# Splitting transposed probabilities straight from PSUM, and moving small steps between VectorE and GpSimd, in a two-layer encoder kernel

## The chip, the cores and the metric

The kernel runs on one core of a Trainium2 chip. The metric is device time of one execution in microseconds (us); runs of the kernel before took 3246.87 us in the median (3243.1 to 3257.06 over 3 runs). Engines are named PE (TensorE, matrix products and transposes), DVE (VectorE), ACT (ScalarE), POOL (GpSimd) and SP (SyncE, which issues the DMAs). PSUM is the memory that PE writes its products to; POOL doesn't read it in this kernel.

## The reference

Input x is 1024 x 1024 in float32. Each of two layers does

```
h    = rmsnorm(x) ; proj = h @ w_in          # 2464 columns for four head groups
A: 4 heads of width 64, 2 key/value heads, normed and rotated q and k, softmax attention
B: 4 heads, differential: softmax(q1 k1 + bias) - lam * softmax(q2 k2 + bias), times v, then a norm
C: 4 heads, low-rank q, k and v, width 96, softmax attention
D: 4 heads, three dilated windows, each with its own softmax, combined by their log-sum-exp
x    = x + concat(A, B, C, D) @ w_out
u    = depthwise width-3 convolution of rmsnorm(x) @ w_up
x    = x + (silu(gate) * val) @ w_down
```

The bias of B and D is a slope times the distance of query and key, -slope * |i - j|, and D also masks keys outside its windows.

## The kernel before, in words

Every matrix product takes operands in fp32r. To keep precision an operand is split into a high part (the value cast to fp32r) and a low part (the value less the high part), and a product is the sum of two or three products of parts.

A layer runs in this order: norm and projection of the columns of B and C (`norm1`, `proj`), then the attention stream, then the MLP. The stream (`stream`, line 414) is a list of events at numbered positions. Within a position events come in the classes SOFT, STEP, SC, EXP, AV, SET, and after them a filler (`fill`): during B the rest of the input projection (`inproj`, for A and D), then the output projection of heads that are done (`out_stage`). Groups come in the order B, C, D, A, with 64, 64, 32 and 64 positions. In B, C and A a pair of query blocks of 128 takes four positions, one step each.

For a pair in B, `sc` (line 645) makes scores of 128 x 1024 in PSUM, in two buffers, for two query blocks and two halves of the head. `mx` (652) adds the bias table, writes P to SBUF and its row maximum, and a second instruction (660) scales the maximum by -slope for the exponential. `ex` (662) is the exponential on ACT with its row sum. `comb` (667), once per query block, at two successive positions, turns sums into factors and adds the second half's P, scaled, to the first (675). In A and C (`dense`, 533) the maximum (550) and the exponential (556) need no bias table. In D (`head_D`, 712) `mx` and `ex` (785, 798) are as in B at 128 x 256, and `finish_D` combines the windows.

`step` (480) is common to all groups. Four transposes by PE put a 128 x 512 piece of P^T in a PSUM bank of the pool `pt` (two buffers; stacks of q and k, line 441, and the small products `o`, line 521, take their banks from the same pool). ACT copies it to `pf` in SBUF. The high part is a cast from `pf` by DVE (492), or for the steps listed in `h_act` a second reading of PSUM by ACT (490). The low part is a subtraction by POOL from `pf` (493). `products` (496) multiplies both parts by v two positions later. `h_act` holds two of four steps in A and B, one of four in C and none in D.

`head_norm` (207) norms q and k: square on ACT, sum on DVE, 1/root on POOL (`rstd`, 108), the product with it on DVE (216), the gain on POOL (218). `by_act` is False while `inproj` runs. `vsplit` (473) splits v: high part on ACT, low part on DVE (helper `split`, line 130).

The order of PE's instructions is the program's (`manual_schedule`, line 1253). The order of DVE, ACT and POOL is drawn up by the framework from its own timeline when the program is built (line 1295). Semaphores are set by the framework.

## Time and profile before

| | |
|---|---|
| runs | 3257.06, 3246.87, 3243.1 us |
| profiled execution | 3249.78 us |
| its span | 3248.0 us |
| PE busy | 3064.0 us, 94% |
| DVE busy | 2042.5 us, 63% |
| ACT busy | 1480.5 us, 46% |
| POOL busy | 1441.2 us, 44% |
| mean granted clock of TensorE | 0.972 |

The profile is of one execution. The span goes from its first to its last instruction. Shares are means over stages that differ much, so the stages are read one by one. A group of instructions in the profile has a line, an engine, an operation, output <- inputs by the program's names, shapes and a count; behind them stand its busy time, the mean time of one, and the idle time of the engine in front of them with what ended it. A row of a stretch holds its start and end, its length, then busy time and number of instructions of PE, PE's weight loads, DVE, ACT and POOL, the mean granted clock, the share of the DMA engines' time and GB/s. A name such as `P<-P,r2b` leaves the buffer's number out.

### The profile page before, as it was taken

The page shows a single profiled execution, that of the slowest core. Times are in us where ns is not written, and L with a number is a line of the kernel's source. Part 1 is how long each engine was busy: PE and PEld are TensorE (multiplying, and loading weights), DVE is VectorE, ACT ScalarE, POOL GpSimd, SP SyncE. Part 2 cuts the span into 40 slices and gives each one's busy share as a digit, 9 for nine tenths or more (in the row PEclk, how much of TensorE's full clock was granted, in tenths as well). Part 3 has the DMA queues.
Part 4 walks back from the last instruction along what each step waited for, and adds up shares of the span by engine and source line. Part 5 has one row for each costly group of instructions (what it writes and reads, how often), then busy time and mean ns, then how long its engine had stood idle before and what let it go on. Part 6 is the DMA issues. An engine that isn't in the chain of part 4 may idle for free. (4 is left out here: it accounts for less than half of the span.)

```text
span 3248.0 us, 44899 instructions
## 1 busy us (share of the span) xinstructions
PE 3064.0 (94%) x16800; PEld 2637.4 (81%) x16800; DVE 2042.5 (63%) x3596; ACT 1480.5 (46%) x2813; POOL 1441.2 (44%) x1128
## 2 busy tenths in 40 slices
PE   7988899799999999999989888997999999999999
PEld 5978888688888888888769788886888888888887
DVE  6789976676734444444566999766767344444445
ACT  5567776556732212222154667765567222221221
POOL 2368775645632222223122677755456322222221
PEclk9999999899999999999999899998999999999999
DMA  4332241221311111111133312412213111111111
GB/s 145 112 105 57 62 132 43 67 62 50 47 54 46 52 46 46 52 46 52 50 113 112 102 51 63 132 44 68 60 49 47 59 39 52 46 52 46 49 49 65
DMA packets 276874, 213.05 MB, mean 66 GB/s; under 512 B 197168, under 2 KB 242608, under 8 KB 276656
## 3 DMA queue, kind: packets, MB, share of 16 engines
q1 hardware_dynamic: 276656, 210.18, 22.4%
q8 instruction: 132, 2.16, 0.3%
q14 instruction: 86, 0.70, 0.1%
HBM read 157.70 MB, written 41.94 MB: 61 GB/s over the span
## 5 line engine op out<-in xcount | busy, mean ns | idle before, releaser
L141 PE MATMUL u<-h2T,wu 128*128 128x512 f32 x4224 | 1013.7, 392 | 0.0
L141 PEld LDWEIGHTS u<-h2T,wu 128*128 128x128 f32 x4224 | 792.3, 188 | 179.8
L493 POOL TENSOR_TENSOR PT<-pf,PT 128x512 fp32r<-128x512 f32 x448 | 599.1, 1342 | 392.3 <-DVE PT L492 240.7
L975 DVE TENSOR_TENSOR xacc<-xacc,d 128x1024 f32<-128x1024 f32 x352 | 424.5, 1217 | 460.2 <-PE d L141 459.7
L141 PE MATMUL d<-wd,gt 128*128 128x512 f32 x2112 | 525.7, 392 | 4.1 <-DVE xacc L975 4.1
L141 PE MATMUL pj<-w,hT 128*128 128x256 f32 (+2 forms) x3072 | 497.5, 316 | 24.7 <-ACT w L134 11.7
L130 POOL TENSOR_TENSOR wu<-rawu,wu 128x1024 fp32r<-128x1024 f32 x88 | 212.6, 2417 | 655.7 <-ACT wu L134 655.7
L141 PEld LDWEIGHTS pj<-w,hT 128*128 128x128 f32 x3072 | 445.2, 197 | 53.9 <-ACT w L134 13.4
L141 PEld LDWEIGHTS d<-wd,gt 128*128 128x128 f32 x2112 | 394.7, 188 | 97.0 <-DVE xacc L975 10.8
L944 ACT ACTIVATE c<-u,cw 128x1024 f32<-128x1024 f32 x88 | 106.3, 1207 | 527.9 <-PE u L141 527.8
L488 ACT COPY pf<-pt 128x512 f32<-128x512 f32 x448 | 261.8, 585 | 134.1 <-PE pt L145 109.9
L145 PE MATMUL pt<-cst,P 128*128 128x128 f32 x1792 | 285.7, 284 | 35.4 <-DVE q L464 13.4
L945 DVE SCALAR_TENSOR_TENSOR c<-u,cw,c 128x1023 f32<-128x1023 f32 x88 | 112.9, 1283 | 297.0 <-ACT c L944 296.9
L141 PEld LDWEIGHTS ot<-PT,v 128*128 128x128 f32 x1664 | 260.5, 196 | 46.2 <-POOL PT L493 15.1
L141 PE MATMUL ot<-PT,v 128*128 128x256 f32 x1664 | 282.0, 291 | 8.1 <-POOL PT L493 8.0
L145 PEld LDWEIGHTS pt<-cst,P 128*128 128x128 f32 x1792 | 219.2, 146 | 60.6 <-DVE q L464 16.4
L130 POOL TENSOR_TENSOR wd<-rawd,wd 128x1024 fp32r<-128x1024 f32 x44 | 105.6, 2400 | 289.6 <-ACT wd L134 289.6
L141 PE MATMUL S<-k,q 96*128 96x512 f32 (+2 forms) x512 | 215.2, 445 | 6.8 <-DMA k<-k 5.8
L492 DVE CAST PT<-pf 128x512 fp32r<-128x512 f32 x288 | 163.6, 568 | 64.9 <-ACT pf L488 58.5
L141 PE MATMUL od<-wo,mT 128*128 128x512 f32 x768 | 201.1, 401 | 2.8 <-DVE mT L1024 1.6
L664 ACT ACTIVATE P<-P,nmb 128x1024 f32<-128x1024 f32 x128 | 147.2, 1151 | 103.1 <-DVE nmb L660 102.7
L550 DVE TENSOR_REDUCE nm<-S 128x1 f32<-128x1024 f32 x128 | 156.2, 1220 | 32.7 <-PE S L141 31.2
(202 smaller groups left out, 4199.3 us busy)
## 6 DMA issues: line engine op xcount, KB each, us to landing
rawu<-in_w_up_dram SPq DMA_DIRECT2D x88, 512.0 KB, 3.3
rawd<-in_w_down_dram SPq DMA_DIRECT2D x44, 512.0 KB, 3.3
rawi<-in_w_in_dram SPq DMA_DIRECT2D x20, 512.0 KB, 3.9
rawo<-in_w_out_dram SPq DMA_DIRECT2D x16, 512.0 KB, 3.3
sC<-cqk SPq DMA_DIRECT2D x16, 384.0 KB, 2.4
ld<-sB SPq DMA_DIRECT2D x24, 256.0 KB, 3.6
sD<-pe SPq DMA_DIRECT2D x48, 128.0 KB, 1.7
ld<-sC SPq DMA_DIRECT2D x16, 384.0 KB, 3.5
```

What stands on the lines that cost most here:

```text
L130: eng.tensor_tensor(dst[1], src, dst[0].bitcast(F32), op=ALU.subtract)
L141: self.nc.tensor.matmul(out, l, r, start=start, stop=stop)
L145: self.nc.tensor.transpose(out, in_, self.ident[:p, :p])
L488: nc.scalar.copy(pf, pt)
L492: nc.vector.tensor_copy(PT[:, 0, :], pf)
L493: nc.gpsimd.tensor_tensor(PT[:, 1, :], pf, PT[:, 0, :].bitcast(F32), op=ALU.subtract)
L550: nc.vector.tensor_reduce(nm, Ps["S", i], axis=AX.X, op=ALU.max, negate=True)
L664: nc.scalar.activation(P, P, AF.Exp, bias=jb["nm", i][:, s:s + 1], scale=slope, accum_out=jb["ss", i][:, s:s + 1])
L944: nc.scalar.activation(c, u, AF.Identity, scale=cw[:, 1, jj:jj + 1], bias=cw[:, 3, jj:jj + 1])
L945: nc.vector.scalar_tensor_tensor(c[:, 1:], u[:, :S - 1], cw[:, 0, jj:jj + 1], c[:, 1:], op0=ALU.mult, op1=ALU.add)
L975: nc.vector.tensor_tensor(xacc[:, t, :], xacc[:, t, :], d, op=ALU.add)
```

## The change

Seven edits:

1. In `step`, ACT casts the high part straight from PSUM for every step, and DVE subtracts it from PSUM for the low part. `pf`, the cast by DVE and the subtraction by POOL go; so does `h_act`. PT has four buffers in place of three.
2. In B and D, the sum of scores and table is multiplied by -slope in the instruction that takes the maximum, which becomes a minimum. It is used as the exponential's bias as it stands; the separate scaling goes (64 instructions per layer in B, 64 in D).
3. `comb` runs once per pair, at the later of its two positions, with two reciprocals of two columns and one narrow product for both query blocks. The two wide products are the same.
4. The product of `head_norm` with 1/root is on POOL while `by_act` is False.
5. The low part of v is on POOL.
6. `finish_D` follows edit 2 (minimum, sign).
7. The tiles of sums and maxima in B are per pair, with two buffers.

```diff
--- before.py
+++ after.py
@@ -213,7 +213,7 @@
         ss = sp.tile([128, nh], F32, tag="hss", name="hss")
         nc.vector.tensor_reduce(ss, sv, axis=AX.X, op=ALU.add)
         r = self.rstd(sp, ss, d, nh, "hr")
-        nc.vector.tensor_tensor(dst, src, bc(r.unsqueeze(2), [128, nh, d]), op=ALU.mult)
+        (nc.vector if self.by_act else nc.gpsimd).tensor_tensor(dst, src, bc(r.unsqueeze(2), [128, nh, d]), op=ALU.mult)
         if gain is not None:
             nc.gpsimd.tensor_tensor(dst, dst, gain, op=ALU.mult)
 
@@ -473,27 +473,22 @@
     def vsplit(self, pos, src, c0, dst, n=NT, tag="v"):
         def go():
             t = (self.dp if n > NT else self.ac).tile([128, n, 128], F32R, tag=tag, name=tag, bufs=1 if n > NT else 2)
-            self.split((t[:, :, 0:64], t[:, :, 64:128]), src["t"][:, :n, c0:c0 + 64])
+            self.split((t[:, :, 0:64], t[:, :, 64:128]), src["t"][:, :n, c0:c0 + 64], "act", "pool")
             dst["t"] = t
         self.ev(pos, self.SET, go)
 
-    def step(self, cols, box, h_act=False):
+    def step(self, cols, box):
 
         nc = self.nc
         pt = self.pt.tile([128, 512], F32, tag="pt", name="pt")
         for o, ap in cols:
             self.T(pt[:, o:o + 128], ap)
         PT = self.ac.tile([128, 2, 512], F32R, tag="PT", name="PT", bufs=self.n_PT)
-        pf = self.ac.tile([128, 512], F32, tag="pf", name="pf", bufs=2)
-        nc.scalar.copy(pf, pt)
-        if h_act:
-            nc.scalar.copy(PT[:, 0, :], pt)
-        else:
-            nc.vector.tensor_copy(PT[:, 0, :], pf)
-        nc.gpsimd.tensor_tensor(PT[:, 1, :], pf, PT[:, 0, :].bitcast(F32), op=ALU.subtract)
+        nc.scalar.copy(PT[:, 0, :], pt)
+        nc.vector.tensor_tensor(PT[:, 1, :], pt, PT[:, 0, :].bitcast(F32), op=ALU.subtract)
         box["PT"] = PT
 
-    def products(self, g, Ps, v, done, h_act, late=0):
+    def products(self, g, Ps, v, done, late=0):
 
 
         lag, nc = 2, self.nc
@@ -502,7 +497,7 @@
             box = {}
             self.ev(g + kp, self.STEP, lambda kp=kp, box=box: self.step(
                 [(kk * 256 + i * 128, Ps[i][:, (2 * kp + kk) * 128:(2 * kp + kk + 1) * 128])
-                 for kk in range(2) for i in range(2)], box, kp in h_act))
+                 for kk in range(2) for i in range(2)], box))
 
             def mms(kp=kp, box=box):
                 if kp == 0:
@@ -570,7 +565,7 @@
                     self.mix_job(h, j, mb["m"][:, 2 * j:2 * j + 2, :])
                 elif j == 3:
                     self.mix_out(h, mb["m"])
-            self.products(gj, Ps, v, done, (1, 3) if C == "A" else (3,))
+            self.products(gj, Ps, v, done)
         return 16
 
     def mix_job(self, h, j, mix):
@@ -650,44 +645,44 @@
                     self.mm(ps[:, ks], qs_[s]["t"][0:96, qb * 128:(qb + 1) * 128], ks_[s]["t"][0:96, ks], True, True)
 
             def mx(i, s, j=j, Ps=Ps, jb=jb):
-                if s == 0:
-                    jb["ss", i] = at.tile([128, 2], F32, tag="ssb", name="ssb", bufs=3)
-                    jb["nm", i] = at.tile([128, 2], F32, tag="nmb", name="nmb", bufs=3)
+                if s == 0 and i == 0:
+                    jb["ss"] = at.tile([128, 2, 2], F32, tag="ssb", name="ssb", bufs=2)
+                    jb["nm"] = at.tile([128, 2, 2], F32, tag="nmb", name="nmb", bufs=2)
                 P = Ps[i, s] = at.tile([128, S], F32, tag="P", name="P", bufs=self.n_P)
-                o, nm = (7 - 2 * j - i) * 128, jb["nm", i][:, s:s + 1]
-                nc.vector.tensor_tensor_reduce(out=P, in0=Ps["S", i, s], in1=self.toep[:, o:o + S], scale=1.0, scalar=NEG,
-                                               op0=ALU.add, op1=ALU.max, accum_out=nm)
-                nc.vector.tensor_scalar(nm, nm, -slope, None, op0=ALU.mult)
+                o = (7 - 2 * j - i) * 128
+                nc.vector.tensor_tensor_reduce(out=P, in0=Ps["S", i, s], in1=self.toep[:, o:o + S], scale=-slope, scalar=-NEG,
+                                               op0=ALU.add, op1=ALU.min, accum_out=jb["nm"][:, s, i:i + 1])
 
             def ex(i, s, Ps=Ps, jb=jb):
                 P = Ps[i, s]
-                nc.scalar.activation(P, P, AF.Exp, bias=jb["nm", i][:, s:s + 1], scale=slope,
-                                     accum_out=jb["ss", i][:, s:s + 1])
-
-            def comb(i, j=j, Ps=Ps, jb=jb):
-                if j == 0 and i == 0:
+                nc.scalar.activation(P, P, AF.Exp, bias=jb["nm"][:, s, i:i + 1], scale=-1.0,
+                                     accum_out=jb["ss"][:, s, i:i + 1])
+
+            def comb(j=j, Ps=Ps, jb=jb):
+                if j == 0:
                     mb["rs"] = at.tile([128, NT], F32, tag="rsb", name="rsb")
-                qb, ss = 2 * j + i, jb["ss", i]
+                ss = jb["ss"]
                 r2 = at.tile([128, 2], F32, tag="r2b", name="r2b")
-                nc.vector.reciprocal(r2, ss)
-                nc.vector.tensor_copy(mb["rs"][:, qb:qb + 1], r2[:, 0:1])
-                nc.vector.scalar_tensor_tensor(r2[:, 1:2], r2[:, 1:2], ss[:, 0:1], self.nlam, op0=ALU.mult, op1=ALU.mult)
-                nc.vector.scalar_tensor_tensor(Ps[i, 0], Ps[i, 1], r2[:, 1:2], Ps[i, 0], op0=ALU.mult, op1=ALU.add)
-                Ps[i] = Ps[i, 0]
+                nc.vector.reciprocal(mb["rs"][:, 2 * j:2 * j + 2], ss[:, 0, :])
+                nc.vector.reciprocal(r2, ss[:, 1, :])
+                nc.vector.scalar_tensor_tensor(r2, r2, self.nlam, ss[:, 0, :], op0=ALU.mult, op1=ALU.mult)
+                for i in range(2):
+                    nc.vector.scalar_tensor_tensor(Ps[i, 0], Ps[i, 1], r2[:, i:i + 1], Ps[i, 0], op0=ALU.mult, op1=ALU.add)
+                    Ps[i] = Ps[i, 0]
             for i in range(2):
                 for s in range(2):
                     p = gj - 8 + 2 * i + s
                     self.ev(p, self.SC, lambda i=i, s=s, sc=sc: sc(i, s))
                     self.ev(p + 1, self.SOFT, lambda i=i, s=s, mx=mx: mx(i, s))
                     self.ev(p + 2, self.EXP, lambda i=i, s=s, ex=ex: ex(i, s))
-                self.ev(gj - 3 + i, self.SOFT - 1, lambda i=i, comb=comb: comb(i))
+            self.ev(gj - 2, self.SOFT - 1, comb)
 
             def done(o, j=j):
                 if j == 0:
                     mb["m"] = at.tile([128, NT, 64], F32, tag="mix", name="mix")
                 nc.vector.tensor_tensor(mb["m"][:, 2 * j:2 * j + 2, :], o,
                                         bc(mb["rs"][:, 2 * j:2 * j + 2].unsqueeze(2), [128, 2, 64]), op=ALU.mult)
-            e = self.products(gj, Ps, v, done, (2, 3), 1)
+            e = self.products(gj, Ps, v, done, 1)
 
         def norm(k):
             if k == 0:
@@ -785,19 +780,17 @@
         def mx(u, n, Pb):
             if n == 0:
                 Pb["P"] = at.tile([128, 4, 256], F32, tag="P", name="P", bufs=self.n_P)
-                Pb["nm"] = at.tile([128, 4], F32, tag="nmd", name="nmd", bufs=3)
             if u < 2:
                 i = 4 * u + n
                 tab, off = sh["t1"], 128 if i == 0 else 0 if i == 7 else 64
             else:
                 tab, off = t2["t"], 128 * (1 - n % 2)
-            nc.vector.tensor_tensor_reduce(out=Pb["P"][:, n, :], in0=Pb["S"][:, n, :], in1=tab[:, off:off + 256], scale=1.0,
-                                           scalar=NEG, op0=ALU.add, op1=ALU.max, accum_out=stat(u, n, 0))
-            nc.vector.tensor_scalar(Pb["nm"][:, n:n + 1], stat(u, n, 0), -slope, None, op0=ALU.mult)
+            nc.vector.tensor_tensor_reduce(out=Pb["P"][:, n, :], in0=Pb["S"][:, n, :], in1=tab[:, off:off + 256], scale=-slope,
+                                           scalar=-NEG, op0=ALU.add, op1=ALU.min, accum_out=stat(u, n, 0))
 
         def ex(u, n, Pb):
             P = Pb["P"][:, n, :]
-            nc.scalar.activation(P, P, AF.Exp, bias=Pb["nm"][:, n:n + 1], scale=slope, accum_out=stat(u, n, 1))
+            nc.scalar.activation(P, P, AF.Exp, bias=stat(u, n, 0), scale=-1.0, accum_out=stat(u, n, 1))
 
         def av(u, rr, Pb, box):
             PT = box["PT"]
@@ -874,12 +867,12 @@
             nv = b["nv"] = n2.rearrange("p (j s b) -> p s b j", s=2, b=2)
             f = b["f"] = at.tile([128, 3, 8], F32, tag="fd", name="fd")
             f1, f2, den = (f[:, i, :] for i in range(3))
-            nc.vector.tensor_tensor(v8(den), v8(m1), nv[:, 0], op=ALU.max)
+            nc.vector.tensor_tensor(v8(den), v8(m1), nv[:, 0], op=ALU.min)
             nc.vector.tensor_tensor(f1, m1, den, op=ALU.subtract)
             nc.vector.tensor_tensor(v8(f2), nv[:, 0], v8(den), op=ALU.subtract)
 
         def fexp():
-            nc.scalar.activation(b["f"][:, 0:2, :], b["f"][:, 0:2, :], AF.Exp, scale=slope)
+            nc.scalar.activation(b["f"][:, 0:2, :], b["f"][:, 0:2, :], AF.Exp, scale=-1.0)
 
         def weights():
             m1, s1, f, nv = b["m1"], b["s1"], b["f"], b["nv"]
@@ -1177,7 +1170,7 @@
             tp = te.enter_context(self.pool(f"tp{l}", bufs=1, side=at))
             self.toep = tp.tile([128, 1920], mybir.dt.float16, name="toep")
             nc.sync.dma_start(self.toep, self.a["toep"])
-            self.n_P, self.n_PT = 6, 3
+            self.n_P, self.n_PT = 6, 4
             st = {"in": self.inproj(l, hT, sp)}
             xes, oe, de = ExitStack(), ExitStack(), ExitStack()
```

## Rows read from the trace of the kernel before

**Rows 1.** Busy time per stretch: B, C, D, A and MLP of layer one, layer two's B, three positions.

```profile
203.60:441.10 237.50, 204.83 (x1421) 189.34 (x1420) 219.12 (x467) 168.02 (x337) 176.17 (x163) 0.93 0.29 85
441.10:597.90 156.80, 146.88 (x960) 131.60 (x959) 106.40 (x192) 105.56 (x213) 97.07 (x76) 0.96 0.21 52
597.90:718.50 120.60, 104.71 (x701) 96.18 (x700) 86.34 (x289) 69.12 (x186) 63.55 (x44) 0.87 0.31 72
718.50:858.10 139.60, 136.26 (x912) 121.27 (x911) 96.52 (x150) 102.65 (x209) 88.28 (x72) 1.00 0.16 43
...
935.10:1610.00 674.90, 673.47 (x2917) 547.23 (x2915) 317.97 (x268) 150.70 (x142) 193.28 (x81) 1.00 0.14 47
...
1825.00:2062.40 237.40, 204.77 (x1421) 188.89 (x1420) 219.52 (x465) 168.11 (x337) 175.63 (x163) 0.93 0.29 85
...
242.80:251.40 8.60, 8.60 (x69) 8.29 (x68) 7.78 (x22) 6.10 (x14) 6.86 (x8) 1.00 0.35 95
```

**Rows 2.** DVE's groups of instructions in B of layer one (203.6 to 441.1 us).

```profile
L658 DVE CUSTOM_DVE_ANT_0 P<-S,toep 128x1024 f32<-128x1024 f32 x57 | 69.1, 1217 | 2.4 <-PE pt L145 0.9
L675 DVE SCALAR_TENSOR_TENSOR P<-P,r2b 128x1024 f32<-128x1024 f32 x31 | 49.3, 1589 | 0.4
L216 DVE TENSOR_TENSOR pe<-pe,hr 128x256 f32<-128x256 f32 (+1 forms) x23 | 18.1, 786 | 0.2 <-POOL hr L123 0.2
L492 DVE CAST PT<-pf 128x512 fp32r<-128x512 f32 x32 | 16.8, 524 | 5.7 <-ACT pf L488 5.7
L674 DVE SCALAR_TENSOR_TENSOR r2b<-r2b,ssb,nlam 128x1 f32<-128x1 f32 x30 | 13.9, 465 | 0.0
L660 DVE TENSOR_SCALAR nmb<-nmb 128x1 f32<-128x1 f32 x58 | 8.1, 143 | 0.3
...
L673 DVE COPY rsb<-r2b 128x1 f32<-128x1 f32 x30 | 4.4, 146 | 0.2
...
L130 DVE TENSOR_TENSOR v<-ld,v 128x512 fp32r<-128x512 f32 x3 | 3.0, 1003 | 0.0
```

**Rows 3.** Line 675 alone, whole run: shortest, median and longest in ns.

```profile
L675 DVE SCALAR_TENSOR_TENSOR P<-P,r2b x64: 1267/1285/2322, 197.3 to 2049.1; 128x1024 f32<-128x1024 f32 x64
```

**Rows 4.** Groups of the whole run: a low part that DVE takes from PSUM.

```profile
L172 DVE TENSOR_TENSOR hT<-ntp,hT 128x512 fp32r<-128x512 f32 x32 | 21.8, 686 | 17.6 <-ACT hT L171 17.4
```

**Rows 5.** ACT's groups in B of layer one.

```profile
L488 ACT COPY pf<-pt 128x512 f32<-128x512 f32 x64 | 37.2, 581 | 17.3 <-PE pt L145 12.3 <-POOL PT L493 3.4 <-POOL hr L123 1.0
L490 ACT CAST PT<-pt 128x512 fp32r<-128x512 f32 x32 | 19.0, 594 | 0.0
```

**Rows 6.** POOL's groups in B of layer one.

```profile
L493 POOL TENSOR_TENSOR PT<-pf,PT 128x512 fp32r<-128x512 f32 x63 | 90.3, 1437 | 35.2 <-DVE PT L492 17.5 <-DVE nmb L660 6.4 <-issue 5.2
...
L218 POOL TENSOR_TENSOR pe<-pe,gDq 128x256 f32<-128x256 f32 x8 | 7.0, 872 | 3.9 <-DVE pe L216 2.3 <-DVE nmb L660 1.6
```

**Rows 7.** PE's waits in B of layer one: total us, times, longest.

```profile
PE S L141 <- DVE nmb L658: 11.2, 10, 2.7
PE stp L145 <- ACT pf L488: 6.7, 5, 2.1
```

**Rows 8.** ACT's waits in B of layer one: total us, times, longest.

```profile
ACT P L664 <- DVE nmb L660: 43.7, 30, 3.1
```

**Rows 9.** Timeline of PE in B: start us, us, four transposes of a step.

```profile
242.84 0.60 PE L145 MATMUL pt<-cst,P 128*128 128x128 f32 x4
```

**Rows 10.** Timeline of DVE in B: start us, us; two instructions in a row.

```profile
307.81 0.14 DVE L660 TENSOR_SCALAR nmb<-nmb 128x1 f32<-128x1 f32 x1
307.88 0.40 DVE L214 TENSOR_REDUCE hss<-sqh 128x4 f32<-128x256 f32 x1
```

**Rows 11.** PE's waits in C of layer one (441.1 to 597.9 us).

```profile
PE pt L145 <- ACT pf L488: 3.6, 1, 3.6
PE ot L141 <- POOL PT L493: 2.7, 3, 1.4
```

**Rows 12.** PE's waits in D of layer one (597.9 to 718.5 us).

```profile
PE pt L145 <- DVE q L464: 6.3, 4, 2.2
```

## What the change should do: a prediction

> **What bounds the kernel now.** I read the busy time per stage first, cut at the first transposes of P of each head group [rows 1]. In the MLP part of the first layer PE is busy 673.5 of 674.9 us and no touched instruction runs; the second layer's is alike, and neither can change. The attention stream is where the change lies, and its four stages have four different limits. In B, VectorE (DVE) is busy 219.1 of 237.5 us (92%), PE only 204.8, and PE's granted clock is 0.93, so it spends spells at 1.2 in place of 2.4 GHz, behind its idle time. The second layer repeats B within 0.1 us. C is near PE's limit (146.9 of 156.8), A is at it (136.3 of 139.6). D is bound by nobody: PE 104.7, DVE 86.3 of 120.6 us, a chain of short dependent steps with a clock of 0.87. ScalarE (ACT) and GpSimd (POOL) are nowhere the fullest. When nothing is late, three positions of B take 8.60 us with PE busy all of it [rows 1], 2.87 us each; the stage needs 3.7 us on average. That gap is DVE's.
>
> Next DVE's groups inside B [rows 2], then who PE waits for there: score products wait for DVE's maxima, stack transposes for ACT's copy out of PSUM [rows 7]. So the question is first what the change does to DVE's 219 us, and then who holds PE's two transpose banks.
>
> **The terms, per layer, stage B.** Removed from DVE: the norm factor products of the in-projection (L216, 18.1 us), the casts of P^T (L492, 16.8 us), the scalings of the maxima (L660, 8.1 us), the copies of 1/sum (L673, 4.4 us), the low parts of v (L130, 3.0 us), and half of the 30 narrow products of L674 (15 x 465 ns = 7.0 us), since one now serves a pair; reciprocals stay two per pair [rows 2]. Together 57.4 us.
>
> Added to DVE: one subtraction per step that reads PSUM and writes 128x512 in fp32r. The same form is in the trace at 686 ns [rows 4]. POOL does 63 of them in this window today [rows 6]; 63 x 0.686 = 43.2 us.
>
> Contention: L675, which reads two SBUF tiles, takes 1285 ns at the median but 1589 ns on average here, 2322 at worst [rows 2, 3], an excess of 31 x 0.304 = 9.4 us. POOL is busy 176.2 us; it loses 90.3 us of low parts and gains 23 products at about 0.87 and 3 low parts of v at 1.44 us [rows 6], which leaves 110. If the excess follows POOL's busy share it falls to 5.9 us, 3.5 us less. The Trainium skill says why the two meet (SBUF — State Buffer, "Who interferes with whom"): a DVE instruction with two SBUF inputs and a GpSimd instruction that reads SBUF want the same read port, and whichever starts first keeps it for the whole instruction. The trace agrees, with 2322 ns against 1267 at best. Were today's low parts the only holders, the whole 9.4 us would go, and the stage's term below would be -17 and not -11 us; but what stays on POOL also reads SBUF, so I keep the share.
>
> Sum of durations: 43.2 - 57.4 - 3.5 = -17.7 us. Durations overlap: an L660 of 0.14 us starts at 307.81 and the next instruction at 307.88 [rows 10], so a short instruction occupies 70 ns less than its row. The change drops 161 instructions and adds 63; 98 x 0.07 = 6.9 us comes back. Net **-11 us**; DVE 219 to 208, still the fullest engine, so I give B -11 us at unchanged idle time. Bounds: -24 (no overlap, whole excess gone) to +9 (with the wait below).
>
> **What I cost at nothing in B.** The ready bias: ACT waits 43.7 us for scaled maxima [rows 8], but ACT is not the limit and DVE hardly waits for it; the exponentials come earlier into slack. Dropping the copy to pf frees ACT (37.2 us of copies against 32 more casts at 594 ns, 19.0 us [rows 5]): hidden likewise. The moved products put POOL at 110 of 237 us; their gain product and rotation queue behind them, shorter than behind today's low parts. No DMA is added, removed or moved on SP's queue, and POOL issues none. The fourth PT buffer takes the room of pf.
>
> **The new wait.** A transpose bank was free when ACT had copied it; now DVE's subtraction frees it, behind whatever stands in DVE's queue: maxima of 1.22 us, or two L675 in a row, because the combination steps of a pair now stand together. PE queues its later transposes, score products and in-projection behind that wait. The trace has no such wait at every step. Bound above: each of 16 pairs waits one more L675, 16 x 1.27 = 20 us, which more than eats the gain. Bound below: a gain, the 6.7 us of waits on ACT's pf [rows 7] going away. I take zero: while PE waits there, DVE is working through its queue, which is already what the stage is charged for.
>
> **C, D, A.** DVE has room. C: 64 subtractions against 48 casts, 43.9 - 25.2 = +18.7, less 4 low parts of v, puts DVE at about 121 of 157 us. A: 64 against 32, 43.9 - 16.8 = +27, less 2 low parts, about 121 of 140. C gains from waits on pf and POOL's low part, 3.6 and 2.7 us [rows 11]; I take -2 (bounds -6, +10). A has only 3.3 us of PE idle time and gets a fuller DVE; I take +1 (bounds -2, +15). D: 64 scalings (143 ns) and 8 low parts of v (about 1.0 us) leave DVE, 32 subtractions cost 0.16 more than casts: -12 us of durations, and each low part of P^T is ready without POOL's 1.4 us. But D's largest wait is a transpose behind the stack's own subtraction, 6.3 us [rows 12], which stays. I take -3 (bounds -10, +4).
>
> Per layer -11 - 2 - 3 + 1 = -15, so **-30 us**. The profiled execution took 3249.78 us (span 3248.0 and 1.8 around it), 2.9 us above the median of 3246.87; so about 3220 in its terms, **3217 us** as a median.
>
> **Rivals.**
> First, **PE becomes the bound of B**. DVE's bursts now stall PE, and with them smaller the stalls and the low clock go together. PE's work at full clock: a mean clock of 0.93 means some 14% of 237.5 us at the lower level, 33 us; half of it is lost, less what was idle anyway, so about 190 us of work. At C's fill of 94% that is 202 us, -35 per layer. With -4 elsewhere: -78, 3169 us. For it: the 2.87 us positions; against: DVE's 208 us.
>
> Second, **the new wait gives B's gain back**: 0.7 us per pair in 16 pairs is the 11 us. The total is -4 per layer, 3239 us. For it: both combination steps stand at one position, right in front of the last two subtractions of the pair before it, and DVE is full; against: it was full before too, with the same S banks waiting for it. The order of DVE, ACT and POOL is drawn up by the framework's own schedule when the program is built, and only PE's is written by hand, so the subtraction may be put ahead of the combination or behind it. That also decides whether the bias really comes early.
>
> Third, **slower: the banks in C and A**. Their positions last 2.45 and 2.18 us. Four transposes 0.60 [rows 9], ACT's cast 0.59 and the subtraction 0.686 make 1.9; behind a maximum over 1024 scores, 1.22 us like L658's, it is 3.1. Where the small product o holds the other bank, once per pair, PE then waits 0.65 and 0.92 us: 16 x 0.65 + 16 x 0.92 = +25 us per layer in place of -1. With B and D as forecast +11 per layer, +22: 3269 us. It decides from about 0.45 us per pair on, where it cancels the gain. For it: A has no slack; against: half of A's and a quarter of C's steps already hold the bank for two ACT instructions (1.18 us), hardly shorter than cast and subtraction, and PE loses almost nothing there.
>
> **Chances.** Forecast 0.52, first rival 0.16, second 0.20, third 0.12. About 0.5% (16 us) is what a measurement of this kernel can tell from no change: faster is below 3230.6, slower above 3263.1. Faster: 0.50 + 0.16 + 0.04 = 0.70; same: 0.02 + 0.15 + 0.03 = 0.20; slower: 0.01 + 0.09 = 0.10. Range 3172 to 3258: it takes in the forecast, the second rival and half of the first, and leaves out most of the third and the lower half of the first.
>
> **What would show it.** Right: B at about 226 us per layer with DVE near 208 and still the fullest; L675's mean near 1.5 us; POOL below 115 us; L660's group gone and ACT's wait on maxima shorter; C and A within 2 us of now; MLP the same. Wrong: PE waits on transposes released by DVE's subtraction of more than some 10 us per layer in B (second rival) or of any size in C and A (third); or B near 202 us with PE at 94% and full clock (first).

## The result and the profile after

The changed kernel takes 3204.61 us in the median of 4 runs (3201.03 to 3204.88) against 3245.87 for the kernel before (4 runs): a ratio of 0.9864, 95% interval 0.984 to 0.9888, some 41 us less. The forecast was 3217. The profiled execution took 3201.03 us, with a span of 3199.2; the stage times below are of the two profiled executions, which lie 49 us apart.

Busy time per stretch of the kernel after, cut as in [rows 1] (columns as there): B, C, D and A of layer one, its MLP, then B, D and A of layer two.

```profile
205.70:435.60 229.90, 198.52 (x1419) 185.00 (x1418) 197.96 (x377) 157.45 (x303) 96.95 (x125) 0.94 0.30 89
435.60:590.10 154.50, 146.96 (x960) 128.75 (x959) 115.52 (x193) 98.05 (x196) 18.66 (x15) 1.00 0.20 51
590.10:691.10 101.00, 91.63 (x701) 83.37 (x700) 80.12 (x228) 70.14 (x187) 32.72 (x20) 1.00 0.38 89
691.10:837.30 146.20, 139.23 (x911) 122.93 (x910) 112.49 (x180) 90.81 (x177) 8.95 (x10) 0.99 0.14 41
...
914.50:1589.00 674.50, 673.06 (x2916) 547.11 (x2915) 317.62 (x267) 150.67 (x142) 192.87 (x81) 1.00 0.14 47
...
1803.60:2029.30 225.70, 198.07 (x1421) 185.19 (x1420) 196.26 (x375) 156.29 (x303) 100.16 (x126) 0.93 0.31 90
...
2184.40:2286.70 102.30, 92.11 (x700) 83.52 (x699) 79.25 (x226) 70.13 (x187) 32.72 (x20) 1.00 0.38 87
2286.70:2431.80 145.10, 138.00 (x911) 121.48 (x910) 112.37 (x179) 91.01 (x177) 8.92 (x10) 1.00 0.14 42
```

Against [rows 1], B fell by 7.6 us in layer one and 11.7 in layer two, C by 2.3, the MLP stayed. D fell by 19.6 us: most of the gain lies in the stage to which the forecast gave 3. A rose by 6.6. In B, DVE's busy time fell by 21 us but the stage only by 7.6: DVE is now 86% full and idle for 31.9 us, where it was idle for 18.4, and PE (198.5 us) is as busy as DVE (198.0).

DVE's groups in B of the kernel after, which answer to [rows 2, 3]:

```profile
L653 DVE CUSTOM_DVE_ANT_0 P<-S,toep 128x1024 f32<-128x1024 f32 x58 | 70.4, 1218 | 13.5 <-PE pt L145 13.2
L488 DVE TENSOR_TENSOR PT<-pt,PT 128x512 fp32r<-128x512 f32 x64 | 43.6, 685 | 5.7 <-ACT PT L487 5.6
L670 DVE SCALAR_TENSOR_TENSOR P<-P,r2b 128x1024 f32<-128x1024 f32 x31 | 40.8, 1328 | 0.5
...
L668 DVE SCALAR_TENSOR_TENSOR r2b<-r2b,nlam,ssb 128x2 f32<-128x2 f32 x15 | 3.6, 241 | 0.5
```

The maximum with the scaling in it costs what it cost without (1218 against 1217 ns), the subtraction its price (685 ns; the forecast had 686). The wide product of the combination fell from 1589 to 1328 ns, the narrow one from 465 to 241. New is the first row's last column: the maxima stood idle 13.2 us until transposes by PE had read a P tile and so set it free; before, such waits were 0.9 us in the same row.

PE's longest waits in B of the kernel after, against [rows 7]:

```profile
PE pt L145 <- DVE PT L488: 9.7, 10, 1.9
PE S L141 <- DVE nmb L653: 9.4, 6, 4.5
```

The first is the new wait that the forecast described, the second has six long waits in place of ten shorter ones. PE also waits behind DVE's subtraction in C and A, where in the kernel before it waited for ACT's reading of a bank for 3.6 us [rows 11] and 0.2 us; C of layer one, then A:

```profile
PE pt L145 <- DVE PT L488: 3.5, 4, 1.2
```

```profile
PE pt L145 <- DVE PT L488: 5.7, 8, 2.3
```

### The profile page after: what moved, and what is told of

Its sections match the earlier page's. It is cut to its first block, busy times and chain, and to the rows that moved or that the text cites. A ratio compares the mean times of both kernels' runs of the same rounds, so it can differ in the third digit from the quotient of the medians.

```text
span 3199.2 us, 44078 instructions
## 1 busy us (share of the span) xinstructions
PE 3031.2 (95%) x16800; PEld 2601.1 (81%) x16800; DVE 2021.4 (63%) x3304; ACT 1424.2 (45%) x2653; POOL 920.5 (29%) x780
## 5 line engine op out<-in xcount | busy, mean ns | idle before, releaser
L968 DVE TENSOR_TENSOR xacc<-xacc,d 128x1024 f32<-128x1024 f32 x352 | 424.7, 1217 | 460.0 <-PE d L141 459.6
L487 ACT CAST PT<-pt 128x512 fp32r<-128x512 f32 x448 | 261.6, 584 | 183.7 <-PE pt L145 175.4
L488 DVE TENSOR_TENSOR PT<-pt,PT 128x512 fp32r<-128x512 f32 x448 | 305.1, 686 | 49.6 <-ACT PT L487 47.0
L145 PE MATMUL pt<-cst,P 128*128 128x128 f32 x1792 | 278.5, 279 | 55.2 <-DVE PT L488 49.4
L145 PEld LDWEIGHTS pt<-cst,P 128*128 128x128 f32 x1792 | 209.7, 142 | 88.7 <-issue 37.8
L141 PE MATMUL ot<-PT,v 128*128 128x256 f32 x1664 | 270.9, 285 | 0.0
L653 DVE CUSTOM_DVE_ANT_0 P<-S,toep 128x1024 f32<-128x1024 f32 x128 | 155.6, 1219 | 27.3 <-PE pt L145 23.2
L134 ACT CAST gt<-c 128x1024 fp32r<-128x1024 f32 x44 | 46.3, 1053 | 283.5 <-POOL c L945 283.5
```

The costliest lines, as they stand in the source:

```text
L134: self.nc.scalar.copy(dst, src)
L141: self.nc.tensor.matmul(out, l, r, start=start, stop=stop)
L145: self.nc.tensor.transpose(out, in_, self.ident[:p, :p])
L487: nc.scalar.copy(PT[:, 0, :], pt)
L488: nc.vector.tensor_tensor(PT[:, 1, :], pt, PT[:, 0, :].bitcast(F32), op=ALU.subtract)
L653: nc.vector.tensor_tensor_reduce(out=P, in0=Ps["S", i, s], in1=self.toep[:, o:o + S], scale=-slope, scalar=-NEG, op0=ALU.add, op1=ALU.min, ...
```

## What happened in D

Timeline of D of the kernel before (start us, us, what; the bracket is the idle time in front and its releaser). One step, from transposes to the next transposes of P:

```profile
612.85 0.65 PE L145 MATMUL pt<-cst,P 128*128 128x128 f32 x4 [1.39 <-DVE q L464]
...
614.71 0.27 DVE L796 TENSOR_SCALAR nmd<-m 128x1 f32<-128x1 f32 x2
614.89 0.51 ACT L800 ACTIVATE P<-P,nmd 128x256 f32<-128x256 f32 x1 [2.31 <-DVE nmd L796]
...
615.40 0.49 ACT L800 ACTIVATE P<-P,nmd 128x256 f32<-128x256 f32 x1
...
615.89 0.56 ACT L488 COPY pf<-pt 128x512 f32<-128x512 f32 x1
...
616.51 0.63 PE L145 MATMUL stp<-cst,ld 128*64 128x128 f32 x4 [1.69 <-ACT pf L488]
...
617.17 0.58 ACT L459 CAST q<-stp 64x512 fp32r<-64x512 f32 x1 [0.72 <-PE stp L145]
...
617.78 0.69 DVE L464 TENSOR_TENSOR q<-stp,q 64x512 fp32r<-64x512 f32 x1 [0.87 <-ACT q L459]
...
618.52 0.47 PE L145 MATMUL pt<-cst,P 128*128 128x128 f32 x1 [1.39 <-DVE q L464]
```

The transposes end at 613.50, but ACT's copy out of the bank stands behind two exponentials that wait for their scaled maxima; it runs at 615.89. Then the next transposes get the bank, ACT casts, DVE subtracts, and only then does the next step begin: 5.7 us, at a granted clock of 0.92. The forecast saw the end of this loop (a transpose behind DVE's subtraction for the stack) and said that it stays. The same kind of step in the kernel after:

```profile
603.10 0.63 PE L145 MATMUL pt<-cst,P 128*128 128x128 f32 x4 [0.29 <-DVE PT L488]
...
603.83 0.59 ACT L487 CAST PT<-pt 128x512 fp32r<-128x512 f32 x1 [0.21 <-PE pt L145]
...
604.83 0.51 ACT L793 ACTIVATE P<-P,m 128x256 f32<-128x256 f32 x1 [0.41 <-DVE m L788]
604.88 0.60 PE L145 MATMUL stp<-cst,ld 128*64 128x128 f32 x4
...
605.05 0.69 DVE L488 TENSOR_TENSOR PT<-pt,PT 128x512 fp32r<-128x512 f32 x1
...
605.88 0.30 PE L145 MATMUL pt<-cst,P 128*128 128x128 f32 x1 [0.40 <-DVE PT L488]
```

The cast runs 0.1 us behind the transposes and ahead of the exponentials, the stack's transposes wait for nothing, and the step takes 2.78 us at full clock (1.00 in D, where it was 0.87). Over all 32 steps of D in layer one, worked out from the timelines, ACT reads the bank 1.25 us behind the transposes on average in the kernel before and 0.22 us in the kernel after; exponentials stand between in 15 steps and in 5.

Much of the gain comes with the clock. PE does the same 701 instructions in 91.6 us of busy time in place of 104.7, while its idle time falls from 15.9 to 9.4 us: 13.1 of D's 19.6 us are PE's busy time, as the granted clock rose from 0.87, part of D at the lower level, to 1.00.

## The experiments

Stage times in us of each run's profiled execution, layer one / layer two, each from the first transposes of P of its group to those of the next, A to its own last; the median is of all executions of the run:

| run | median | B | C | D | A |
|---|---|---|---|---|---|
| before | 3245.87 | 237.4 / 237.4 | 156.8 / 159.2 | 120.6 / 119.7 | 139.6 / 139.7 |
| changed | 3204.61 | 230.0 / 225.7 | 154.5 / 155.1 | 100.9 / 102.3 | 146.2 / 145.1 |
| e1 split alone | 3196.58 | 221.6 / 224.4 | 158.4 / 158.5 | 100.5 / 100.3 | 144.9 / 144.9 |
| e2 all but the split | 3238.05 | 228.7 / 224.8 | 154.6 / 156.4 | 125.0 / 126.0 | 140.0 / 140.2 |
| e3 scaling back | 3256.44 | 257.0 / 257.6 | 154.1 / 156.4 | 102.0 / 99.9 | 146.3 / 146.1 |
| e4 norm and v back | 3209.40 | 223.3 / 222.3 | 159.7 / 159.4 | 101.3 / 103.9 | 146.4 / 147.7 |
| e5 steps per block | 3177.64 | 209.5 / 213.4 | 154.9 / 157.0 | 100.9 / 105.9 | 147.7 / 146.3 |
| e6 three PT | 3223.21 | 226.4 / 221.5 | 155.5 / 156.6 | 111.6 / 116.8 | 147.6 / 146.1 |
| e7 seven P, three PT | 3222.91 | 223.8 / 226.1 | 154.9 / 154.7 | 109.7 / 111.2 | 144.6 / 146.7 |
| e8 w_out on GpSimd | 3194.99 | 227.7 / 221.4 | 154.1 / 155.5 | 101.7 / 106.5 | 141.4 / 141.5 |
| e9 e5 and e8 | 3161.75 | 211.1 / 211.6 | 153.9 / 155.1 | 101.8 / 106.0 | 142.0 / 141.4 |
| e11 e5, scaling back | 3179.47 | 214.7 / 216.3 | 154.6 / 157.9 | 98.7 / 99.3 | 146.4 / 146.5 |
| e12 e5, norm back | 3200.30 | 216.6 / 217.3 | 155.8 / 157.6 | 101.6 / 103.5 | 148.7 / 146.2 |

The order of DVE, ACT and POOL is drawn up anew at every build. Stages that an edit touches little or not at all moved by 2 to 4 us per layer (B in e8, where four of DVE's 377 instructions move; D of layer two in e5, whose edit is in B alone), so differences of that size are not explained here.

**e1, the split alone.** The kernel before with

```diff
-        pf = self.ac.tile([128, 512], F32, tag="pf", name="pf", bufs=2)
-        nc.scalar.copy(pf, pt)
...
-        nc.gpsimd.tensor_tensor(PT[:, 1, :], pf, PT[:, 0, :].bitcast(F32), op=ALU.subtract)
+        nc.scalar.copy(PT[:, 0, :], pt)
+        nc.vector.tensor_tensor(PT[:, 1, :], pt, PT[:, 0, :].bitcast(F32), op=ALU.subtract)
...
-            self.n_P, self.n_PT = 6, 3
+            self.n_P, self.n_PT = 6, 4
```

> The kernel before with one part of the change: P^T split from PSUM by ScalarE and VectorE (four PT buffers), nothing else. Theory 1 (the other parts pay in B, the split pays in D): B gets slower, since VectorE gains 63 subtractions of 0.69 us and loses 32 casts of 0.52 us: +8 to +15 us per layer; D keeps nearly all of its gain, 100 to 106 us per layer in place of 120; A +5, C -2; in all 3225 to 3255 us. Theory 2 (the early bias and the moved low parts of v pay in D): D stays at 115 to 121 us and the whole is 3260 to 3290 us, slower than before.

Measured: 3196.58 us, ratio 0.9843 (0.9828 to 0.9857), at least as fast as the whole change. D has all of its gain, as theory 1 has it. But B got faster too, by 13 to 16 us per layer, where 8 to 15 were to be lost. Its stretches of B and D:

```profile
205.40:427.00 221.60, 193.25 (x1420) 179.01 (x1419) 212.62 (x499) 154.47 (x305) 81.19 (x100) 0.98 0.31 91
...
585.40:685.90 100.50, 91.49 (x700) 83.54 (x699) 82.93 (x289) 69.17 (x187) 22.06 (x12) 1.00 0.37 86
```

DVE does all subtractions and yet is busy for 6.5 us less than before (212.6 against 219.1): the wide product takes 1307 ns, the narrow one 228 and the norm factor product 436, where they took 1589, 465 and 786 beside POOL's low parts. And DVE is 96% full, idle for 9.0 us in place of 18.4.

**e2, all but the split.** The changed kernel with the old `step` and three PT buffers, e1's edit in reverse.

> The changed kernel with the split of P^T as it was (copy to pf, cast by VectorE, low part on GpSimd, three PT buffers); the other parts stay. Theory 1: D falls back to 115 to 121 us per layer, A returns to 140; B is limited by GpSimd, which then has about 200 us of work there: 205 to 218 us; in all 3185 to 3215 us. Theory 2: D keeps 100 to 106 us per layer, and the whole is 3150 to 3180 us, faster than the changed kernel.

Measured: 3238.05 us, ratio 0.9964 (0.9947 to 0.9981). D is at 125, above even its old time, and A at 140: both belong to the split, as theory 1 has it. I expected POOL to hold B, and it does not: it is busy for 187.9 of 228.6 us, and DVE is idle for 38.6 us there. e1 and e2 together would give 61 us, the whole change gives 41: the parts get in each other's way, and the place is B.

**e3, scaling back.** The changed kernel with the separate scaling in B and D, the step per pair kept:

```diff
-                nc.vector.tensor_tensor_reduce(out=P, in0=Ps["S", i, s], in1=self.toep[:, o:o + S], scale=-slope, scalar=-NEG,
-                                               op0=ALU.add, op1=ALU.min, accum_out=jb["nm"][:, s, i:i + 1])
+                nc.vector.tensor_tensor_reduce(out=P, in0=Ps["S", i, s], in1=self.toep[:, o:o + S], scale=1.0, scalar=NEG,
+                                               op0=ALU.add, op1=ALU.max, accum_out=nm)
+                nc.vector.tensor_scalar(nm, nm, -slope, None, op0=ALU.mult)
...
```

> The changed kernel with the maxima scaled by an instruction of their own again (64 per layer in B, 64 in D); the rest stays. Theory 1: VectorE gets some 70 ns per scaling back: B +4, D +2 us per layer, in all about +12 us, 3215. Theory 2: D goes back by 12 us or more per layer, 3235 us or more.

Measured: 3256.44 us, ratio 1.0034 (1.0019 to 1.005): the whole gain is gone. Neither theory had the place: D does not move, B rises by 27 and 32 us per layer. DVE is busy for only 205.7 of 257.0 us there. ACT's longest wait in B, then DVE's two:

```profile
ACT P L660 <- DVE nmb L656: 39.3, 20, 5.0
...
DVE P L654 <- PE pt L145: 18.5, 13, 3.5
DVE r2b L669 <- ACT P L660: 10.7, 13, 1.3
```

In the kernel after the three are 11.7, 13.2 and 4.2 us. I read it as a chain: the exponentials wait for scalings that stand behind other work in DVE's queue, the combination waits for the exponentials, and the next maxima wait for P tiles. The scaling itself starts no later than elsewhere, 1.0 us behind its maximum on average here, in the kernel before and in e11 below, and ACT's wait is no longer than in the kernel before [rows 8]; what differs is that the step per pair waits for it.

**e4, norm factor products and low parts of v back on DVE.**

```diff
-        (nc.vector if self.by_act else nc.gpsimd).tensor_tensor(dst, src, bc(r.unsqueeze(2), [128, nh, d]), op=ALU.mult)
+        nc.vector.tensor_tensor(dst, src, bc(r.unsqueeze(2), [128, nh, d]), op=ALU.mult)
...
-            self.split((t[:, :, 0:64], t[:, :, 64:128]), src["t"][:, :n, c0:c0 + 64], "act", "pool")
+            self.split((t[:, :, 0:64], t[:, :, 64:128]), src["t"][:, :n, c0:c0 + 64])
```

> The changed kernel with the norm factor products and the low parts of v back on VectorE. Theory 1: B +12 to +18 us per layer (VectorE's 198 us become about 213), D up to +3; in all 3230 to 3245 us. Rival: VectorE's idle time in B, which rose to 32 us, takes it up: less than +5 us per layer, under 3215 us.

Measured: 3209.40 us, ratio 0.9889 (0.9868 to 0.9909). The rival: B did not rise, it fell by 3 to 7 us although DVE has 8.7 us more to do; C lost 4 to 5. So in the changed kernel DVE's load does not set B's time.

**e5, the combination per query block.** What is left to suspect in B is the step per pair.

```diff
...
-                for i in range(2):
-                    nc.vector.scalar_tensor_tensor(Ps[i, 0], Ps[i, 1], r2[:, i:i + 1], Ps[i, 0], op0=ALU.mult, op1=ALU.add)
-                    Ps[i] = Ps[i, 0]
+                nc.vector.scalar_tensor_tensor(Ps[i, 0], Ps[i, 1], r2, Ps[i, 0], op0=ALU.mult, op1=ALU.add)
+                Ps[i] = Ps[i, 0]
...
-            self.ev(gj - 2, self.SOFT - 1, comb)
+                self.ev(gj - 3 + i, self.SOFT - 1, lambda i=i, comb=comb: comb(i))
```

> The changed kernel with the combination steps per query block again, at two successive positions; the rest of the change stays. Theory P (the step per pair keeps all four tiles of P one position longer, and VectorE then waits for a free one of the six: 13.2 us per layer in B): that wait falls under 4 us and B to 210 to 221 us per layer, the whole to 3170 to 3192 us, faster than the changed kernel and than the split alone. Rival (the step per pair saves instructions and costs nothing): B rises by the some 60 small instructions to 230 to 235 us, the whole to 3205 to 3220 us.

Measured: 3177.64 us, ratio 0.9786 (0.9765 to 0.9808). Theory P's numbers came: B at 209.5 and 213.4 us, and the wait for P tiles from 13.2 to 2.9. The stretch of B and that wait:

```profile
207.00:416.50 209.50, 190.06 (x1421) 177.51 (x1420) 198.84 (x418) 155.07 (x303) 103.39 (x124) 0.98 0.33 97
```

```profile
DVE P L653 <- PE pt L145: 2.9, 6, 1.0
```

DVE has 41 instructions more than in the changed kernel and is busy 0.9 us longer, and the stage is 20 us shorter (12 in layer two). The edit undoes two things at once, the merging and the later position of the first query block.

**e6 and e7, buffers.** The changed kernel with three PT buffers; and with three PT buffers and seven P tiles (SBUF has no room for seven beside four PT buffers).

```diff
-            self.n_P, self.n_PT = 6, 4
+            self.n_P, self.n_PT = 6, 3
```

```diff
-            self.n_P, self.n_PT = 6, 4
+            self.n_P, self.n_PT = 7, 3
```

> The changed kernel with three PT buffers in place of four. Theory S (D pays because the split itself frees the bank and the low part sooner): D stays at 100 to 104 us per layer, the whole within 8 us of the changed kernel. Rival (D pays because of the fourth buffer: there a step's PT is read three positions later): D goes back to 110 us or more per layer, the whole to 3225 us or more.

> The changed kernel with seven P tiles in place of six and, for room, three PT buffers. Theory P: VectorE's wait for transposes to free a P tile goes from 13.2 to under 4 us per layer in B, and B to 212 to 222 us; C, D and A as with three PT buffers. Rival: B stays within 4 us of the run with three PT buffers and six P tiles.

e6 measured 3223.21 us, ratio 0.9924 (0.9898 to 0.995): the rival in D, the whole 2 us under its bound. D goes back to 111.6 and 116.8 us. Its stretch of D in layer one, and ACT's longest wait in it:

```profile
589.60:701.30 111.70, 95.89 (x701) 86.59 (x700) 80.01 (x230) 68.26 (x187) 33.06 (x20) 0.97 0.34 80
```

```profile
ACT PT L487 <- PE ot L141: 16.9, 15, 2.6
```

ACT's cast waits for the products with v to free a PT tile, and holds the bank while it does. In the changed kernel this wait is not among those of D. ACT reads the bank 1.72 us behind the transposes on average here, later than in the kernel before, but for another reason.

e7 measured 3222.91 us, ratio 0.9922 (0.9895 to 0.9948). The rival, nearly: B is 2.6 us under e6 in layer one and 4.6 us over it in layer two. The wait for transposes is gone, but others stand in its place, DVE's in B:

```profile
DVE rsb L666 <- ACT P L658: 6.0, 7, 1.3
DVE r2b L667 <- ACT P L658: 5.9, 8, 1.2
```

So theory P is right about the culprit, the step per pair, and wrong about the means: the P tiles alone are not what it costs, as a seventh buys nothing. The step per pair starts only when the fourth exponential is done and then puts two wide products in a row. Which of the two costs more was not separated, so by what path the step per pair costs its time stays open.

**e8, low parts of w_out on GpSimd.** In A, where PE waits 5.7 us per layer behind DVE's subtraction, the longer of two such places per layer (2.28 and 1.78 us) looks like this in the kernel after (DVE's timeline, then PE's):

```profile
800.05 0.95 DVE L130 TENSOR_TENSOR wo<-rawo,wo 128x256 fp32r<-128x256 f32 x1
800.93 1.21 DVE L545 TENSOR_REDUCE nm<-S 128x1 f32<-128x1024 f32 x1
802.06 0.74 DVE L130 TENSOR_TENSOR wo<-rawo,wo 128x256 fp32r<-128x256 f32 x2
802.73 1.27 DVE L488 TENSOR_TENSOR PT<-pt,PT 128x512 fp32r<-128x512 f32 x2
```

```profile
803.55 0.63 PE L145 MATMUL pt<-cst,P 128*128 128x128 f32 x4 [2.28 <-DVE PT L488]
```

```diff
-                self.split((w[:, 0, c:c + 256], w[:, 1, c:c + 256]), raw[:, c:c + 256], "act", "dve" if c % 512 else "pool")
+                self.split((w[:, 0, c:c + 256], w[:, 1, c:c + 256]), raw[:, c:c + 256], "act", "pool")
```

> The changed kernel with all low parts of w_out on GpSimd (half of them are on VectorE). Theory W (A's 6 us per layer are lost at two places where VectorE works on w_out in front of a subtraction that holds a transpose bank, 2.1 us each): A falls by 3 to 5 us per layer to 141 to 143 us, the whole by 6 to 12 us to 3193 to 3199. Rival (A's loss lies with the subtraction's 0.69 us itself at every step): A stays at 144 us or more and the whole within 4 us of the changed kernel.

Measured: 3194.99 us, ratio 0.9836 (0.9808 to 0.9864); A at 141.4 and 141.5: theory W. The two waits shrink to 0.6 and 1.0 us, and the row as a whole:

```profile
PE pt L145 <- DVE PT L488: 3.1, 8, 1.0
```

POOL, busy for 9 us in A, had the room.

**e9, e5 and e8 together.**

> The changed kernel with the combination steps per query block and the low parts of w_out on GpSimd, the two edits that paid one by one. If they add up: B 209 to 215, A 141 to 143 us per layer, the whole 3166 to 3174 us, faster than either alone (3177.6 and 3195.0). If A's gain depends on where the order of the queues falls: A stays at 146 us and the whole at 3175 to 3180.

Measured: 3161.75 us, ratio 0.9724 (0.9706 to 0.9742), the fastest of all and 4 us under the range. B and A are within 2 us of where each edit alone put them.

**e11, steps per block and the scaling back.** e3's edit on top of e5.

> The changed kernel with the combination steps per query block and the maxima scaled by an instruction of their own. Theory K (the early bias is worth much only where the step per pair has to wait for the fourth exponential; there it was worth some 30 us per layer in B): with steps per block B is 212 to 222 us, 3 to 9 us more than with the early bias, and the whole 3182 to 3196 us. Rival (the early bias is worth 30 us wherever it stands): B 236 us or more, the whole 3225 us or more.

Measured: 3179.47 us, ratio 0.9778 (0.9762 to 0.9794). Theory K, and the whole even lower than it: with steps per block the early bias is worth 5 and 3 us per layer in B, with the step per pair 27 and 32. The 5 and 3 us are no more than DVE's busy time rose by (6.6 and 3.4), and of the size by which builds differ, so no worth of being early is seen there. As D was 2 to 7 us shorter here, the whole is no slower than e5 (0.9778 against 0.9786).

**e12, steps per block and the norm factor products back on DVE.** The first half of e4's edit on top of e5.

> The changed kernel with the combination steps per query block and the norm factor products back on VectorE (the low parts of v stay on GpSimd). Theory V (with steps per block VectorE is again the fullest engine of B, 199 of 209.5 us, and its load sets the time): its 16 us more per layer make B 219 to 227 us, the whole 3195 to 3212 us. Rival (as with the step per pair, where taking the products back cost nothing in B): B at most 214 us, the whole under 3185 us.

Measured: 3200.30 us, ratio 0.9841 (0.9824 to 0.9859). Theory V in direction and in the whole, but B rose by 7 and 4 us, not by 10 to 18: DVE's busy time rose by 6.4 us (198.8 to 205.3), because the products, which cost 786 ns each beside the old low parts on POOL, cost 391 now. B's rise is half of the 23 us between the medians. The two profiled executions lie only 16 us apart, with 11 in B; what makes up the rest of the medians' distance stays open.

**e10, the fourth PT buffer alone.** The kernel before with

```diff
-            self.n_P, self.n_PT = 6, 3
+            self.n_P, self.n_PT = 5, 4
```

> The kernel before with four PT buffers and, for room, five P tiles in place of six; P^T is split as before. Only D is read: there one P tile serves two positions, so five are plenty, while B must get slower. If the fourth buffer alone makes D's gain: D 100 to 108 us per layer. If the split is needed beside it (the copy to pf and GpSimd's 1.4 us still stand in the chain): D 114 to 121 us.

Measured in a single execution: D at 116.2 and 115.0 us. So the buffer without the split is worth some 4 to 5 us per layer, the change without it 3 to 9 (e6), both together 17 to 20: the loop opens only when both links go. Without the split ACT's copy still starts 1.17 us behind the transposes on average. Beside it, B with five P tiles takes 310 us in place of 237: one P tile fewer costs B much, one more bought nothing in e7.

## Why the prediction was right, and where its steps failed

The time, 12 us under the forecast, is inside the range, and faster was the likeliest case. That the sum is so near is in part luck: D gave 14 to 17 us more per layer than forecast, A took 4 to 6 more, and B's nearness hides two errors; the stages of the profiled executions sum to -23 and -28 us per layer, where the forecast had -15. Of the signs that the forecast set itself, the scalings' group, POOL's 97 us and ACT's shorter wait for maxima (11.7 us for 43.7) came; DVE near 208 us, the wide product near 1.5 us and C and A within 2 us did not, and its sign of the third rival, waits behind the subtraction in C and A, came too. By its steps:

**B, -11 forecast, -7.6 and -11.7 measured: the sum held because two errors cancelled.** DVE's busy time fell by 21.2 us, not 11. The step that was off is the one that let the excess of the wide product follow POOL's busy share (5.9 of 9.4 us left): 31 x (1328 - 1285) = 1.3 us was left, and the narrow products (465 to 241 ns) and the rotations (L229, 347 to 235 ns) got cheaper too. The Trainium skill (SBUF — State Buffer, "Who interferes with whom") has the holder as any GpSimd instruction that reads SBUF. The trace agrees that some of POOL's instructions make DVE wait, but not that all do alike: POOL was still busy for 97 us and the excess nearly ended, and in the whole run of the kernel after 17 of the 64 wide products started while one of POOL's small powers (L123, 128x4 or 128x8) was running, and had no excess. In B of layer one before, 7.1 of the 9.4 us fall on the 9 of 31 wide products that started while a low part of P^T was running on POOL. Taking the low parts of P^T off POOL (e1) ends the excess, and making every other part of the change but leaving them there (e2) keeps most of it; e1's wide and narrow product, then e2's:

```profile
L670 DVE SCALAR_TENSOR_TENSOR P<-P,r2b 128x1024 f32<-128x1024 f32 x31 | 40.5, 1307 | 0.6
...
L669 DVE SCALAR_TENSOR_TENSOR r2b<-r2b,ssb,nlam 128x1 f32<-128x1 f32 x30 | 6.8, 228 | 0.0
```

```profile
L675 DVE SCALAR_TENSOR_TENSOR P<-P,r2b 128x1024 f32<-128x1024 f32 x31 | 47.0, 1530 | 0.5
...
L673 DVE SCALAR_TENSOR_TENSOR r2b<-r2b,nlam,ssb 128x2 f32<-128x2 f32 x15 | 6.4, 429 | 0.5
```

So the low parts of P^T were most of what counted, and the reading that the forecast gave as -17 was the better one. The other error is "at unchanged idle time": it rose from 18.4 to 31.9 us. The forecast booked the combination per pair as a saving of small instructions and feared it for the transpose banks; it costs 12 to 20 us per layer (e5), with waits for late exponentials and for P tiles, whose shares were not separated.

Stage length less DVE's busy time in B of layer one shows it in one line. All but e2 have the split. Steps per block: e1 9.0, e11 9.2, e5 10.7, e12 11.3, e9 12.5 us. Step per pair: e4 16.6, e7 23.5, e6 28.5, e8 31.4, the change 31.9, e2 38.6, e3 51.3 us. In layer two the two groups are 12 to 14 and 16 to 52 us. The kernel before, with steps per block but without the split, has 18.4. With the split and steps per block DVE's work sets B, as the forecast had it; with the step per pair it does not.

**The early bias, costed at nothing.** Right with steps per block, as far as e11 can tell. In the change as made it saves B from some 30 us per layer that the step per pair would cost without it (e3).

**The new wait, taken as zero.** PE waited 9.7 us for transposes behind the subtraction, at the forecast's own mark of some 10 for the second rival, and no more for ACT's copy of pf. That rival's wait is there; its sum is not, as DVE had more relief than it was given.

**C, -2 forecast, -2.3 and -4.1 measured.** Near in size, but not for the reason given, the waits on pf and on POOL's low part: the split alone ends these, puts 5.6 us of waits behind the subtraction in their place, and leaves C at 158.4 and 158.5 (e1), where it was 156.8 and 159.2. The gain hangs on the low parts of v: with them on POOL and without the split C is at 154.6 and 156.4 (e2), with them back on DVE at 159.7 and 159.4 (e4). Why they matter so much there was not followed further.

**A, +1 forecast, +6.6 and +5.4 measured.** Mis-sized, against bounds of -2 and +15. The third rival's mechanism works here, not at every pair but at two places per layer, where w_out's low parts stand in front of the subtraction (e8).

**D, -3 forecast, -19.6 and -17.4 measured: the term that was missed.** The forecast named the wait behind the stack's subtraction as the largest and as staying. It was the end of a loop that ran through ACT's copy behind two exponentials. And it costed the fourth PT buffer at nothing, as it "takes the room of pf": a step's PT is read three positions later in D, so with three buffers the cast waits for them and holds a bank; in e6 the buffer is worth 11 and 15 us per layer there. Nor had D's term anything for the clock, which rose from 0.87 to 1.00.

## What to carry to other kernels

Before a step is merged to save instructions, ask which tiles it now holds longer and which last input it waits for: the step per pair saved 41 instructions on a nearly full engine and cost up to 20 us per layer. A stage that no engine fills may be a loop: write out one turn of it from the timeline, with the place in each queue where the links stand, before saying which wait stays. And where a part is undone by itself, look at the stages and not only at the sum: here the split alone gave -51 us and the rest alone -10 (3196.58 and 3238.05 against 3247.85 beside them), of a change worth -41.

## What the runs showed of the hardware

An instruction on DVE that reads two SBUF tiles was up to twice as dear beside POOL's subtractions as without them: 465 against 228 ns for the narrow product, 1589 against 1307 for the wide one, on average, in two kernels that have both in the same form (before and e1). The excess sits in a few instructions: the wide product's median was 1285 ns beside them and 1282 in the kernel after. A cost read from a row of such an instruction is that of its neighbour too, and goes when the neighbour goes.
